# Program order and paced softmax steps in the attention region of a hybrid decoder trunk

## The chip, the cores and the metric

The kernel runs on one core of a Trainium2 chip. The metric is the device time of one execution in microseconds (us). TensorE (PE in the profile) multiplies matrices, VectorE (DVE), ScalarE (ACT) and GpSimd (POOL) do the element-wise work, and SyncE (SP) issues nearly all DMA transfers. Each engine works through its own queue of instructions in order, and semaphores order the engines against each other. An instruction that waits at the head of its queue holds all that stand behind it.

## The reference

Two layers over 1024 tokens of width 1024, in float32. Each layer modulates and normalizes its input, projects it once, gives the columns to three groups of heads, gates each group's output, projects back and adds to the input. The group that the change touches is A, the sliding-window attention; B is a chunked retention, C a gated linear attention.

```python
h = rms_norm(x, pre_gain) * (1.0 + scale) + shift
proj = h @ w_in
(aq, ak, av, ag, rq, rk, rv, rg, gq, gk, gv, gg, ga) = jnp.split(proj, IN_SPLITS, axis=-1)
aq = apply_rotary(aq.reshape(B, S, ATTN_HEADS, HEAD_DIM), positions, rope_freq)
ak = apply_rotary(ak.reshape(B, S, ATTN_KV_HEADS, HEAD_DIM), positions, rope_freq)
a_out = sliding_window_attention(aq, ak, av, sinks) * jax.nn.silu(ag)
...
y = jnp.concatenate([a_out, r_out, g_out], axis=-1) @ w_out
return x + gate * rms_norm(y, post_gain)
```

Attention has 8 query heads of 64 and 2 key/value heads; each query sees the 128 keys up to its own, so a block of 128 queries needs its own block of keys and the one before:

```python
s = jnp.where(valid[None, :, None, None], s, -1e30)
p = jax.nn.softmax(jnp.concatenate([s, sink], axis=-1), axis=-1)[..., :-1]
o = jnp.einsum('bnhgqk,bnkhd->bnqhgd', p.astype(v.dtype), vv)
```

## The kernel before

The tokens lie in eight tiles of 128. Products of full precision are split: each operand becomes a high part in a fast float32 format and a low part (the rest), and three passes (`PASSES`) of matmuls add high by high, high by low and low by high. Weights come as chunks of 128 x 512 in staging tiles (`st`), and are converted on the chip into high and low parts in a large tile (`arena`) by the function `load`; in the last layer the output weights are combined first (`sw_first`, `sw_split`, lines 568 to 603), since the last output projection uses sums of weight blocks (W00, T1, W11, W10 and others).

*Two kinds of order.* A planner in Python writes the program. It keeps a model of PE's clock (`clk`), which each matmul advances. Work beside the stream of projection matmuls is written as generators (jobs). A job yields either a delay on that clock, mostly out of the table `L` by a key (`lat("aq4", l)`; keys with `@1` are for layer 1), or the name of a flag it needs; `pump`, called between pieces of matmuls, lets every job run whose time has come. The whole trunk stands under `tc.manual_schedule(engines={PE})`: PE executes in the order in which the program is written. The other four engines' order is set by a scheduler, with hints: `tc.high_priority()`, and `tc.issue_after(x)`, which keeps what it encloses behind instruction x.

*Pools.* Temporaries `t` (`t2`) of 128 x 512: 10 buffers; staging tiles: 5; score tiles `smx` (128 x 8 x 129, the 129th column for the sink): 3; PSUM: 3 banks `mm`, 5 banks `aux`. A new tile waits until the last reader of the buffer's earlier tile is done.

*The attention region of a layer.* After the projections of B and C the stream projects keys and values (`do_kv`, a pair of token tiles each; job `attn_kv`, L846), the queries (`attn_rot`, L859, twice per half of the tokens: rotary products with tables that it loads, sums L875/L876, copy L881 and four shifted copies by DMA into `mx`), and then the gate (units ag0 and ag1; `gate`, L1671: tanh on ScalarE L1674, product on VectorE L1675, store to `gS` in DRAM). Along with these run the attention blocks, one job `attn_q` (L952) per 128 queries, started by `attn_run`:

1. `attn_split` (L908): q into high and low parts (ScalarE L913, VectorE L914). For block t+1 it is written behind the scores of block t.
2. scores: 24 matmuls into four `aux` banks.
3. `soft` (L917): copies of the previous block's scores (ScalarE), masked copies of the own block's (VectorE L925), the maximum (L927), eight exponentials with sums (ScalarE L930), the reciprocal (L933), the scaling of all rows (GpSimd L935).
4. `turn` (L938): transposes on VectorE (L940), a difference of values (L943) and four masked products on GpSimd (L948, tile `pr`).
5. AV products: 40 small matmuls (fewer in block 0) into four `aux` banks. They are written after the scores of block t+1 (`("sc", l, t + 1)`) and 17.0 us by the planner's clock after step 3.
6. Eviction: four copies on VectorE (L1011) into a `t` tile, with a store to `aoS`. `turn` of block t+1 is written inside this step, behind the last copy.
7. Once the gate of the half is there: loads of `aoS` and `gS` (key "lao"), the product (VectorE L1030), its split (a cast, VectorE L152, and the difference, GpSimd L1037) and stores to `mixS`; in the last layer the later blocks go to `mixF` whole. Helper lines: L166 matmul, L181 transpose, L150 ScalarE copy, L152 VectorE cast, L155 DMA on SP.

In the same stretch jobs convert output weights (`loader`, L476; chunks L527/L528 and L537), and a job computes the next layer's modulation by products of `w_mod` rows (`mod_third`, L366/L368 into `acc`). The weight loader keeps up to `LAG + 1` chunks in flight: it yields 1.2 us after each issue or conversion.

SP issues all of these transfers from one queue, in the scheduler's order.

## Time and profile before

| | us |
|---|---|
| median of 3 runs | 1026.82 (1024.66 to 1029.02) |
| the profiled execution | 1028.49 |
| its span, first to last instruction | 1026.7 |
| PE busy | 961.7 (94% of the span) |
| VectorE busy | 710.1 (69%) |
| ScalarE busy | 378.5 (37%) |
| GpSimd busy | 278.4 (27%) |
| mean clock granted to TensorE | 0.967 |

The span leaves out what lies before the first and behind the last instruction, 1.8 us here. Busy time is averaged over stages that have different limits; a row of a timeline gives start, duration, engine, line, operation, tiles written <- read, how many instructions it stands for, and in brackets the idle time before it with what released it. A row of the waits gives the waiting engine and line, the engine and line waited for, the total, the number of waits and the longest. The clock granted to TensorE is a share of full speed.

### The profile page before, as it was taken

How to read it: one execution, taken by the hardware profiler on the slowest of the kernel's cores; microseconds unless marked ns; L12 is line 12 of the kernel's file. 1: busy time of each engine (PE TensorE's matmuls, PEld its weight loads, DVE VectorE, ACT ScalarE, POOL GpSimd, SP SyncE). 2: the span in 40 equal slices, each digit the busy share in tenths (PEclk: the TensorE clock that was granted, in tenths of full speed). 3: DMA queues.
4: the chain of work that ended last, by engine and by line, in shares of the span. 5: the costliest groups of instructions: out<-in, count | busy, mean ns of one | idle time of the engine just before them, and what ended most of it. 6: DMA issues, size and time to landing. Idle time of an engine off the chain costs nothing. (4 is left out here: it accounts for less than half of the span.)

```text
span 1026.7 us, 21283 instructions
## 1 busy us (share of the span) xinstructions
PE 961.7 (94%) x7965; PEld 833.2 (81%) x7965; DVE 710.1 (69%) x1692; ACT 378.5 (37%) x1088; POOL 278.4 (27%) x319
## 2 busy tenths in 40 slices
PE   5899999999999997797999999999999998988996
PEld 1699999888988875575889999988998887766775
DVE  3889857687657886564488276774775586777876
ACT  2576312234314443322355232133332344454221
POOL 2322011233211254341114101122331043556200
PEclk8899999999999999799999999999999998988999
DMA  9743414433453447787646151351234334697884
GB/s 316 278 134 123 128 43 149 130 112 97 132 167 97 135 137 233 213 240 273 217 129 195 51 166 37 113 170 63 73 110 136 112 102 129 221 288 237 271 277 138
DMA packets 115527, 163.58 MB, mean 159 GB/s; under 512 B 13232, under 2 KB 56796, under 8 KB 115424
## 3 DMA queue, kind: packets, MB, share of 16 engines
q1 hardware_dynamic: 109728, 152.66, 47.4%
q10 hardware_dynamic: 5696, 9.56, 2.5%
q8 instruction: 63, 1.03, 0.4%
q14 instruction: 40, 0.33, 0.1%
HBM read 118.66 MB, written 41.42 MB: 156 GB/s over the span
## 5 line engine op out<-in xcount | busy, mean ns | idle before, releaser
L166 PE MATMUL mm<-arena 128*128 128x256 f32 (+2 forms) x1824 | 300.1, 321 | 1.8 <-ACT arena L708 1.5
L166 PE MATMUL mm<-arena,arena 128*128 128x256 f32 (+2 forms) x1824 | 296.3, 317 | 0.0
L166 PEld LDWEIGHTS mm<-arena 128*128 128x128 f32 x1824 | 259.7, 193 | 25.7 <-ACT arena L708 1.8
L166 PEld LDWEIGHTS mm<-arena,arena 128*128 128x128 f32 x1824 | 254.7, 189 | 24.0 <-issue 2.2
L639 POOL TENSOR_TENSOR sm<-sm,mhalf 128x1 f32<-128x1 f32 (+1 forms) x64 | 55.7, 870 | 332.2 <-DVE sm L638 324.1
L166 PE MATMUL mm<-arena,mx 128*128 128x512 f32 (+1 forms) x564 | 134.9, 395 | 5.0 <-DMA mx<-mixS 3.1
L166 PEld LDWEIGHTS mm<-arena,mx 128*128 128x128 f32 x564 | 103.3, 192 | 30.6 <-issue 3.6
L150 ACT ACTIVATE arena<-st 128x512 fp32r<-128x512 f32 x94 | 55.6, 627 | 65.0 <-PE mm L166 30.8
L537 POOL TENSOR_TENSOR arena<-st,arena 128x512 fp32r<-128x512 f32 x31 | 43.5, 1406 | 119.2 <-ACT arena L150 108.1
L930 ACT ACTIVATE smx<-smx,sm 128x129 f32<-128x129 f32 x128 | 49.7, 390 | 40.9 <-DVE sm L927 40.9
L537 DVE TENSOR_TENSOR arena<-st,arena 128x512 fp32r<-128x512 f32 x77 | 57.7, 770 | 4.0 <-ACT arena L150 2.8
L368 DVE SCALAR_TENSOR_TENSOR acc<-st,c_act,acc 128x512 f32<-128x512 f32 x60 | 47.2, 787 | 16.4 <-DMA st<-in_w_mod_dram 15.9
L181 PE MATMUL aux<-c_ident,t 128*128 128x128 f32 (+1 forms) x292 | 48.9, 285 | 9.1 <-DVE t L670 8.8
L948 POOL TENSOR_TENSOR pr<-smx,c_dmask 32x256 f32<-32x256 f32 x56 | 44.6, 797 | 35.3 <-DVE smx L940 28.4
L166 PE MATMUL aux<-kT,t 64*128 64x256 f32 (+1 forms) x384 | 33.5, 316 | 20.1 <-DVE t L1011 14.6
L935 POOL TENSOR_TENSOR smx<-smx,sm 128x1024 f32<-128x1024 f32 x16 | 31.6, 1976 | 75.2 <-DVE sm L933 56.9
L166 PEld LDWEIGHTS aux<-kT,t 64*128 64x128 f32 x384 | 28.7, 214 | 26.9 <-DVE t L1011 16.6
L181 PEld LDWEIGHTS aux<-c_ident,t 128*128 128x128 f32 (+1 forms) x292 | 35.2, 145 | 17.1 <-DVE t L670 11.7
L150 ACT ACTIVATE t<-aux 128x256 fp32r<-128x256 f32 (+2 forms) x60 | 25.3, 447 | 63.3 <-PE aux L181 63.2
L166 PEld LDWEIGHTS aux<-t,mx 32*128 32x128 f32 (+1 forms) x896 | 39.5, 187 | 3.8 <-issue 2.1
L702 ACT ACTIVATE t<-aux,mod,mod 128x128 f32<-128x128 f32 x68 | 25.9, 460 | 43.2 <-PE aux L181 14.8
L1063 ACT ACTIVATE t<-aux 128x256 f32<-128x256 f32 x32 | 12.3, 383 | 78.4 <-PE aux L166 71.1
(225 smaller groups left out, 1414.0 us busy)
## 6 DMA issues: line engine op xcount, KB each, us to landing
st<-in_w_in_dram SPq DMA_DIRECT2D x96, 256.0 KB, 3.9
st<-in_w_mod_dram SPq DMA_DIRECT2D x64, 256.0 KB, 3.1
mx<-mixS SPq DMA_DIRECT2D x20, 512.0 KB, 5.7
st<-in_w_last_dram SPq DMA_DIRECT2D x36, 256.0 KB, 3.3
mixS<-t SPq DMA_DIRECT2D x64, 128.0 KB, 1.9
mixS<-t SPq DMA_DIRECT2D x26, 256.0 KB, 3.5
wm<-in_w_mod_dram SPq DMA_DIRECT2D x12, 512.0 KB, 5.4
t<-in_x_dram SPq DMA_DIRECT2D x24, 256.0 KB, 5.4
```

The source lines that it names most:

```text
L150: A.activation(dst, src, AF.Copy)
L166: T.matmul(dst, lhsT, rhs, start=start, stop=stop)
L181: T.transpose(dst, src, idn)
L368: V.scalar_tensor_tensor(acc, wt, c_act[:, k:k + 1], acc, ALU.mult, ALU.add)
L537: e.tensor_tensor(lo, st, f(hi), ALU.subtract)
L639: G.tensor_tensor(r, r, mhalf[:, :w], ALU.pow)
L702: A.activation(hf[:, ks], at[kt], AF.Identity, scale=gain, bias=shift)
L930: A.activation(sm[:, h, :], sm[:, h, :], AF.Exp, bias=mx[:, h:h + 1], accum_out=sums[:, h:h + 1])
L935: eng("pn").tensor_tensor(ph, ph, rs.unsqueeze(2).to_broadcast((P, 8, P)), ALU.mult)
L948: eng(f"pr{i}").tensor_tensor(pr[rr], pb[rr, :, i, :], dmask[rr].unsqueeze(1).to_broadcast((32, 8, 32)), ALU.mult)
L1063: A.activation(sq, po, AF.Square)
```

## The change

It has five parts.

1. From `do_kv(2)` to the last gate projection of each layer the program now stands in an inner `tc.manual_schedule(engines=ORDERED)`, with VectorE, ScalarE, GpSimd and SP: there these engines too execute in the order in which the program is written. `one[0]` tells the functions that they are inside. The hints have no say there; `issue_after` around the gate product is left away inside, those around the rotary tables and `turn` altogether.
2. `soft` becomes `masked`, `exps` and `normed`, each written after a pause (3.8 and 3.9 us of the planner's clock, then 2.4). `turn` follows in the block's own job as soon as the previous block's AV products are written, and no longer inside the eviction; the AV products come 5.4 us after it and no longer wait for the next block's scores. `attn_split` of the next block is written behind `masked`.
3. The AV eviction writes into the block's own score tile (its first four head slots) and not into a `t` tile; its store is written 2.4 us later.
4. Weight chunks: inside, the loader yields 2.0 us per step (`LD`), and the modulation's product is written 4.0 us after its load instead of at once.
5. Smaller pauses (the head norms' and the import of `nullcontext` are left out of the diff): the rotary tables are loaded once per half (`attn_tab`) and not once per unit; the sums and the copies become a job (`attn_swap`) with pauses of 2.4 and 1.4; the gate is a job with 2.0 before its store; the store of v stands behind the rotary step of k; the head norms of B and C yield 2.6 between statistics and product; the gate product's stores come 3.2 behind it.

PE's order stays as the planner writes it. In the new file the lines are shifted: masks L939, maximum L941, exponentials L947, reciprocal L953, scaling L955, transposes L960, masked products L968, eviction L1035, gate product L1052, its difference L1058, gate L1700/L1701, modulation L371.

```diff
--- before.py
+++ after.py
...
@@ -159,6 +159,7 @@
 
 
     clk = [0.0]
+    one = [False]
     jobs = []
     flags = {}
 
@@ -362,11 +363,14 @@
             for k in range(KT):
                 wt = stage()
                 dma("lwm", wt, w_mod[l, j, hh, :, k, :])
+                if one[0]:
+                    yield lat("mod2", l)
                 if k == 0 and j < 2:
                     V.tensor_scalar(acc, wt, c_act[:, k:k + 1], None, ALU.mult)
                 else:
                     V.scalar_tensor_tensor(acc, wt, c_act[:, k:k + 1], acc, ALU.mult, ALU.add)
-                yield lat("mod2", l)
+                if not one[0]:
+                    yield lat("mod2", l)
             yield lat("mod3", l)
             pm = aux()
             if j < 2:
@@ -482,10 +486,10 @@
                 while flying and sum(len(s) for _, s in flying) + n > LAG + 1:
                     convert()
                 flying.append((conv, issue()))
-                yield lat("ld1", l)
+                yield LD if one[0] else lat("ld1", l)
             else:
                 convert()
-                yield lat("ld2", l)
+                yield LD if one[0] else lat("ld2", l)
         loading[0] = False
 
     loading = [False]
@@ -846,25 +850,25 @@
     def attn_kv(l, t, pk):
         kr = t1()[:, 0:P]
         v = gp.tile([P, P], F32, tag="va", name=nm("va"), bufs=2)
-        i = A.activation(v, pk[:, 128:256], AF.Copy)
-        if t in (2, 6):
-            kv["at"] = i
-        dma("sv", vS[t], v)
+        A.activation(v, pk[:, 128:256], AF.Copy)
         rotary(kr, pk[:, 0:128], 2, t, 0)
         yield lat("kv1", l)
+        dma("sv", vS[t], v)
         pt = aux()
         transp(pt[:, 0:P], kr, ident)
         split(kv["kT"][0][:, t * P:(t + 1) * P], kv["kT"][1][:, t * P:(t + 1) * P], pt[:, 0:P])
         flag(("kT", l, t), lat("kv2", l))
 
-    def attn_rot(l, hf, g, w_):
-
-
+    def attn_tab(hf):
         sn, cs = t2(), t2()
         for s, d in ((0, sn), (1, cs)):
-            with tc.issue_after(kv["at"].ins):
-                nc.sync.dma_start(d.rearrange("p (s n) -> p s n", s=2),
-                                  tabS[2 * hf:2 * hf + 2, :, s, :].rearrange("s p n -> p s n"))
+            nc.sync.dma_start(d.rearrange("p (s n) -> p s n", s=2),
+                              tabS[2 * hf:2 * hf + 2, :, s, :].rearrange("s p n -> p s n"))
+        return sn, cs
+
+    def attn_rot(l, hf, g, w_, tab):
+
+        sn, cs = tab
         u, w = [t2(), t2()], [t2(), t2()]
         for c in range(2):
             pm = mm()
@@ -872,17 +876,27 @@
             V.tensor_tensor(u[c], pm, cs, ALU.mult)
             V.tensor_tensor(w[1 - c], pm, sn, ALU.mult)
             pump()
+        if g == 0:
+            kv[hf] = mix_tile(F32).rearrange("p a k q -> p (a k q)").rearrange("p (k n) -> p k n", k=4)
+        job(attn_swap(l, hf, g, u, w))
+
+    def attn_swap(l, hf, g, u, w):
+
         V.tensor_tensor(u[0], u[0], w[0], ALU.subtract)
         V.tensor_tensor(u[1], u[1], w[1], ALU.add)
-        if g == 0:
-            kv[hf] = mix_tile(F32).rearrange("p a k q -> p (a k q)").rearrange("p (k n) -> p k n", k=4)
+        if one[0]:
+            yield 2.4
         for j in range(2):
             q = kv[hf][:, 2 * g + j]
             A.activation(q, u[j], AF.Copy)
+        if one[0]:
+            yield 1.4
+        for j in range(2):
+            q = kv[hf][:, 2 * g + j]
             for r in range(2):
                 dst, src = 64 * r + 32 * (1 - j), 64 * r + 32 * j
                 dma("qst", q[dst:dst + 32], u[1 - j][src:src + 32])
-        flag(("q", l, hf, g), lat("aq6", l))
+        flag(("q", l, hf, g), lat("aq6", l) - (3.8 if one[0] else 0.0))
 
     def attn_v(p):
 
@@ -914,7 +928,7 @@
             eng("qsl").tensor_tensor(qs[1], qt, f(qs[0]), ALU.subtract)
         kv["qs"][t] = qs
 
-    def soft(t, n, pss, sm):
+    def masked(t, n, pss, sm):
 
         for g in range(2):
             for r in range(2):
@@ -925,10 +939,16 @@
                 V.copy_predicated(sv, curmask.unsqueeze(1).to_broadcast((P, 2, P)), pv[:, :, n // P - 1, :])
         mx = small(8)
         V.tensor_reduce(mx, sm, AX.X, ALU.max, negate=True)
+        return mx
+
+    def exps(sm, mx):
         sums = small(8)
         for h in range(8):
             A.activation(sm[:, h, :], sm[:, h, :], AF.Exp, bias=mx[:, h:h + 1],
                          accum_out=sums[:, h:h + 1])
+        return sums
+
+    def normed(sm, sums):
         rs = small(8)
         V.reciprocal(rs, sums)
         ph = sm[:, :, 0:128]
@@ -970,23 +990,28 @@
                         mult(pss[g][r][:, j * n:(j + 1) * n], qs[a][rr, 2 * g + j], kv["kT"][b][rr, cols],
                              i == 0, i == 2, n / 4600.0)
         flag(("sc", l, t))
-        if t + 1 < NT and flags.get(("q", l, (t + 1) // 4, 1), 1e9) <= clk[0]:
-            attn_split(t + 1)
         if t % 4 == 3:
             flag(("s", l, t // 4))
         with tc.high_priority():
-            soft(t, n, pss, sm)
-            if t == 0:
-                turn(t, sm)
-        kv["sm"] = sm
+            mx = masked(t, n, pss, sm)
+        if t + 1 < NT and flags.get(("q", l, (t + 1) // 4, 1), 1e9) <= clk[0]:
+            attn_split(t + 1)
+        yield lat("ax1", l)
+        with tc.high_priority():
+            sums = exps(sm, mx)
+        yield lat("ax2", l)
+        with tc.high_priority():
+            normed(sm, sums)
+        yield lat("ax3", l)
+        if t:
+            yield (0.0, ("av", l, t - 1))
+        with tc.high_priority():
+            turn(t, sm)
+        flag(("tn", l, t))
         pb = sm[:, :, 0:128].rearrange("p h (j b) -> p h j b", j=4)
         cur, prev = kv[("v", t // 2)], kv[("v", max(t - 1, 0) // 2)]
         tc_, tp = t % 2, (t - 1) % 2
         yield lat("aq4", l)
-        if t + 1 < NT:
-            yield (0.0, ("sc", l, t + 1))
-        if t:
-            yield (0.0, ("tn", l, t))
         vd, pr = kv["m"] if t else (None, None)
         po = [aux() for _ in range(4)]
         for s in range(5 if t else 4):
@@ -1004,20 +1029,17 @@
                         w_ = cur[rr, 4 * tc_ + j, cc] if j < i or t == 0 else prev[rr, 4 * tp + j, cc]
                         x = pb[rr, r:8:2, j, :]
                     mult(d3, w_, x, s == 0, s == (4 if t else -i % 4 if i < 2 else 3), 0.03)
-        ao = t2()
-        av = ao.rearrange("p (h q) -> p h q", h=4)
+        av = sm[:, 0:4, 0:128]
         with tc.high_priority():
             for i in range(4):
                 last = V.tensor_copy(av[:, :, 32 * i:32 * i + 32], po[i][:, 0:128].rearrange("p (h a) -> p h a", h=4))
-            if t + 1 < NT:
-                with tc.issue_after(last.ins):
-                    turn(t + 1, kv["sm"])
-                flag(("tn", l, t + 1), 0.0)
         kv["ev"] = last
         flag(("av", l, t))
-        dma("sao", aoS[t], av)
         if t in (2, 4):
             attn_v(t // 2 + 1)
+        if one[0]:
+            yield 2.4
+        dma("sao", aoS[t], av)
         yield (0.0, ("av", l, min(t + 1, NT - 1)))
         for k in range(4):
             yield (0.0, ("g", l, t // 4, k))
@@ -1026,17 +1048,21 @@
         for d, src in ((av, aoS), (gt.rearrange("p (k q) -> p k q", k=4), gS)):
             dma("lao", d, src[t])
         yield lat("ag1", l)
-        with tc.issue_after(kv["ev"].ins):
+        with nullcontext() if one[0] else tc.issue_after(kv["ev"].ins):
             V.scalar_tensor_tensor(ao, gt, 0.5, ao, ALU.mult, ALU.mult)
             whole = l == DEPTH - 1 and t >= PLAIN
-            if whole:
-                dma("sm0", mixF[t, :, 0:4, :], av)
-            if not whole or t % 2 == 0:
+            split_ = not whole or t % 2 == 0
+            if split_:
                 mh, ml = t2(F32R), t2(F32R)
                 copy("mg", mh, ao)
                 eng("mgl").tensor_tensor(ml, ao, f(mh), ALU.subtract)
-                for a, m in ((0, mh), (1, ml)):
-                    dma(f"sm{a}", mixS[t, :, a, 0:4, :], f(m).rearrange("p (k q) -> p k q", k=4))
+        if one[0]:
+            yield 3.2
+        if whole:
+            dma("sm0", mixF[t, :, 0:4, :], av)
+        if split_:
+            for a, m in ((0, mh), (1, ml)):
+                dma(f"sm{a}", mixS[t, :, a, 0:4, :], f(m).rearrange("p (k q) -> p k q", k=4))
         for k in range(4):
             flag(("mix1", l, t, k), lat("lay1", l))
 
...
@@ -1659,13 +1687,11 @@
         do_kv(0)
         do_gv(3)
         do_kv(1)
+        tab = attn_tab(0)
         for g in range(2):
-            attn_rot(l, 0, g, used(l, f"aq{g}"))
+            attn_rot(l, 0, g, used(l, f"aq{g}"), tab)
             pump()
         job(attn_run(l))
-        for p in range(2, NP_):
-            do_kv(p)
-        load(l, "ag0")
         mx = {}
 
         def gate(g, hf, kk, pm):
@@ -1673,35 +1699,43 @@
             th = t2()
             A.activation(th, pm, AF.Tanh, scale=0.5)
             V.scalar_tensor_tensor(th, th, 1.0, pm, ALU.add, ALU.mult)
+            yield 2.0
             dma("sg", gS[4 * hf:4 * hf + 4, :, k].rearrange("t p q -> p t q"), th.rearrange("p (t q) -> p t q", t=4))
             flag(("g", l, hf, k), lat("ag2", l))
 
...
+        one[0] = True
+        with tc.manual_schedule(engines=ORDERED):
+            do_kv(2)
+            do_kv(3)
+            load(l, "ag0")
+            tab = attn_tab(1)
             for g in range(2):
+                attn_rot(l, 1, g, used(l, f"aq{g}"), tab)
+                pump()
+                if l == DEPTH - 1 and g == 0:
+                    sw_first("W00")
+                else:
+                    load(l, ("o3", "ag1")[g])
+            for hf in range(2):
+                for g in range(2):
+                    for kk in range(2):
+                        pm = mm()
+                        project_T(pm, l, hf, used(l, f"ag{g}"), kk * P)
+                        job(gate(g, hf, kk, pm))
+                        pump()
+                    if hf and not g:
+                        if l == DEPTH - 1:
+                            sw_first("W10")
+                        else:
+                            load(l, "o2")
+                if not hf:
                     if l == DEPTH - 1:
+                        sw_first("T1")
+                        sw_first("W11")
                     else:
+                        load(l, "o0")
+                        load(l, "o1")
+        one[0] = False
@@ -1743,8 +1777,10 @@
...
-L = {
...
-"aq4": 17.0,
...
-"aq4@1": 17.0,
...
+L = {
...
+"ax1": 3.8, "ax1@1": 3.8, "ax2": 3.9, "ax2@1": 3.9, "ax3": 2.4, "ax3@1": 2.4, "aq4": 5.4,
...
+"aq4@1": 5.4,
...
 CHUNK = 7
+LD = 2.0
+ORDERED = {mybir.EngineType.DVE, mybir.EngineType.Activation, mybir.EngineType.Pool, mybir.EngineType.SP}
 LAG = 2
 FIN = 1
 
```

More of the change, by code (lines that the diff above doesn't have):

```diff
@@ L1 @@
 import math
-from contextlib import ExitStack
+from contextlib import ExitStack, nullcontext
 import numpy as np
@@ L1066, in head_norm_gate @@
         r = rstd_of(ss, 4, scale, eps)
+        if one[0]:
+            yield 2.6
         g1 = t1()
@@ L1069, in head_norm_gate @@
         eng("hng").tensor_tensor(g1, g1, gate, ALU.mult)
-        yield lat("hn1", l)
+        yield lat("hn1", l) - (2.6 if one[0] else 0.0)
         pt = aux()
```

25 lines of the change are left out of this document (1 added, 24 removed).

## The prediction

> **What bounds the kernel now.** I read the engines' busy time first, then stretches of 50 us, then the tensor engine's waits by line, then the single instructions around each wait. The page:
>
> ```profile
> PE 961.7 (94%) x7965; PEld 833.2 (81%) x7965; DVE 710.1 (69%) x1692; ACT 378.5 (37%) x1088; POOL 278.4 (27%) x319
> ```
>
> PE is the bound, with 65 us of idle time (1026.7 - 961.7). The stretches (start:end, then busy time of PE, PEld, DVE, ACT, POOL, the clock granted to TensorE, DMA share, GB/s) show where that idle time is:
>
> ```profile
> 350.00:400.00 50.00, 44.01 (x448) 35.05 (x448) 36.80 (x65) 22.44 (x76) 20.37 (x19) 0.96 0.54 164
> 400.00:450.00 50.00, 38.94 (x403) 30.82 (x402) 36.05 (x60) 17.85 (x69) 26.05 (x25) 0.83 0.78 226
> ...
> 850.00:900.00 50.00, 44.70 (x461) 35.05 (x449) 34.26 (x63) 22.86 (x79) 24.35 (x24) 0.91 0.57 182
> 900.00:950.00 50.00, 41.18 (x326) 32.11 (x326) 38.04 (x59) 22.89 (x76) 30.57 (x27) 0.85 0.84 264
> 950.00:1000.00 50.00, 48.04 (x272) 37.28 (x271) 40.37 (x73) 14.92 (x33) 7.23 (x8) 0.97 0.83 275
> ```
>
> The attention region of layer 0 lies at about 318 to 436 us, that of layer 1 at about 815 to 945, so the change touches just the stretches with idle time. What PE waited for, first between 355 and 440, then between 855 and 990:
>
> ```profile
> PE aux L166 <- DVE t L1011: 7.0, 3, 4.0
> PE aux L166 <- ACT t L913: 5.6, 1, 5.6
> PE aux L166 <- DVE smx L925: 4.5, 2, 4.3
> ```
>
> ```profile
> PE aux L166 <- DVE t L1011: 11.7, 4, 4.1
> PE aux L166 <- DVE smx L925: 2.4, 2, 1.2
> PE mm L166 <- DVE t L1435: 1.9, 1, 1.9
> ```
>
> Layer 0 loses 7.0 + 5.6 + 4.5 = 17.1 us, layer 1 loses 16.0, of which 4.1 is its last wait on L1011 and 1.9 the output stage. So 10.0 lies before that. PE stands for the copy that clears the AV banks (L1011), the masks that clear the score banks (L925) and the split of q (L913): VectorE's and ScalarE's queues, not their load.
>
> A stall also costs clock. The loss in a stretch is busy time times (1 - clock). Layer 0: 44.01 x 0.04 + 38.94 x 0.17 = 8.4 us, 0.49 per us of idle time. Layer 1: 44.70 x 0.09 + 41.18 x 0.15 + 48.04 x 0.03 = 11.6 us over 16.0, 0.73 per us. I price a microsecond of stall at 1.49 us in layer 0 and 1.73 in layer 1.
>
> What stands in front of L1011? PE's stalls and, below, VectorE's instructions around them:
>
> ```profile
> 398.94 1.43 PE L166 MATMUL aux<-kT,t 64*128 64x256 f32 x14 [4.00 <-DVE t L1011]
> ...
> 432.08 0.58 PE L166 MATMUL aux<-kT,t 64*128 64x256 f32 x1 [5.58 <-ACT t L913]
> 433.66 1.22 PE L166 MATMUL aux<-kT,t 64*128 64x256 f32 x8 [1.00 <-DVE t L1011]
> ```
>
> ```profile
> 943.16 1.22 PE L166 MATMUL aux<-arena,mx 128*128 128x512 f32 x2 [4.14 <-DVE t L1011]
> ```
>
> ```profile
> 397.27 0.75 DVE L528 SCALAR_TENSOR_TENSOR arena<-st,gnc,arena 128x512 fp32r<-128x512 f32 x1 [4.19 <-ACT arena L527]
> ...
> 398.60 0.88 DVE L1011 COPY t<-aux 128x128 f32<-128x128 f32 x4
> ...
> 401.13 1.90 DVE L1030 SCALAR_TENSOR_TENSOR t<-t,t 128x512 f32<-128x512 f32 x2
> 402.95 0.91 DVE L152 CAST t<-t 128x512 fp32r<-128x512 f32 x1
> 403.79 1.18 DVE L1030 SCALAR_TENSOR_TENSOR t<-t,t 128x512 f32<-128x512 f32 x1
> 404.90 1.52 DVE L152 CAST t<-t 128x512 fp32r<-128x512 f32 x1
> ```
>
> ```profile
> 429.15 0.69 DVE L1030 SCALAR_TENSOR_TENSOR t<-t,t 128x512 f32<-128x512 f32 x1 [3.70 <-issue]
> 429.76 1.22 DVE L927 TENSOR_REDUCE sm<-smx 128x8 f32<-128x1032 f32 x1
> 430.90 0.42 DVE L152 CAST t<-t 128x512 fp32r<-128x512 f32 x1
> ```
>
> ```profile
> 940.76 0.69 DVE L603 TENSOR_TENSOR st<-st,st 128x512 f32<-128x512 f32 x1 [3.88 <-DMA st<-in_w_last_dram]
> ...
> 942.82 0.88 DVE L1011 COPY t<-aux 128x128 f32<-128x128 f32 x4
> ```
>
> Each time a step whose data had not come stood at the head of VectorE's queue: a weight piece (4.19 and 3.88 us), a gate product (3.70, with the reduction that the exponentials need behind it). The change orders these queues by hand, so it decides what stands there next.
>
> **The change, part by part** (line numbers of before). Durations of the steps, between 300 and 480 us:
>
> ```profile
> L930 ACT ACTIVATE smx<-smx,sm 128x129 f32<-128x129 f32 x64 | 24.9, 390 | 27.2 <-DVE sm L927 27.2
> L948 POOL TENSOR_TENSOR pr<-smx,c_dmask 32x256 f32<-32x256 f32 x28 | 22.0, 784 | 19.3 <-DVE smx L940 16.3 <-DVE smx L957 1.4
> ...
> L368 DVE SCALAR_TENSOR_TENSOR acc<-st,c_act,acc 128x512 f32<-128x512 f32 x16 | 14.4, 899 | 7.8 <-DMA st<-in_w_mod_dram 7.5
> ...
> L925 DVE COPY_PREDICATED smx<-c_curmask,aux 128x256 f32<-128x256 int32 x32 | 11.9, 439 | 2.0 <-ACT smx L150 1.8
> ...
> L1037 POOL TENSOR_TENSOR t<-t,t 128x512 fp32r<-128x512 f32 x8 | 11.3, 1416 | 14.2 <-DVE t L152 10.3 <-DVE t L1030 2.8 <-issue 0.6
> ...
> L940 DVE STREAM_TRANSPOSE smx<-smx 128x1024 f32<-128x1024 f32 x8 | 9.9, 1238 | 4.3 <-POOL smx L935 4.3
> ```
>
> Weight pieces converted 2.0 us per step, and the modulation product 4.0 us after its load: this removes the wait of the first kind. By the emitted order two or three steps, 4 to 6 us, now lie between issue and conversion. Against the landing times of the page
>
> ```profile
> st<-in_w_in_dram SPq DMA_DIRECT2D x96, 256.0 KB, 3.9
> ...
> st<-in_w_mod_dram SPq DMA_DIRECT2D x64, 256.0 KB, 3.1
> ...
> st<-in_w_last_dram SPq DMA_DIRECT2D x36, 256.0 KB, 3.3
> ```
>
> that is enough while SP's queue is short. The stall of 4.00 at 398.94 goes, and with it the 7.5 us in which VectorE waited for modulation loads, which cost PE nothing where no L1011 was behind.
>
> The eviction into the score tile frees one of ten temporaries per block; L913 had waited for such a slot. It holds the score tile until its store has landed, some microseconds that three such tiles cover; its copies stay (0.88 for four). The store now reads pieces of 512 bytes; no row shows such a store, so I bound it between nothing and one landing of a plain one, and take nothing, since the product that reads it back comes a block later. Rotary tables loaded once per half save four loads per layer on SP, which hide beside projections. The later stores (v, gate, mix) and the pieces of the head norm cost nothing on PE as long as 3 to 7 us of projection matmuls stand before the reader; without that cover each would cost its added pause, 2.0 to 3.2.
>
> Now the new order, block by block. After the last transposes a block needs 1.24 + 4 x 0.78 = 4.4 us before its AV products; the plan gives 5.4, so 1.0 is spare.
>
> Layer 0. AV(4): three gate products with casts (3 x (0.69 + 0.42) = 3.3 on VectorE) and three splits on GpSimd (3 x 1.42 = 4.3) now stand between the q split of block 6 and the transposes and diagonal products of block 4. The GpSimd work starts a cast later than VectorE's, so the delay is 1.1 + 4.3 - 1.0 = 4.4 if nothing stretches, 3.3 - 1.0 = 2.3 if GpSimd's part falls beside other work, 6 if they stretch as in the rows at 401 to 405; I take 5. Scores(7): the second half of AV(5)'s eviction stands behind the reciprocal of block 6, which needs its reduction (1.2) and eight exponentials (8 x 0.39 = 3.1), and the reduction stands behind a weight cast that waits for its load. That is at least 3 us and at most what it was (5.58 + 1.00); I take 5.5. AV(1) and AV(5): one or two steps of 0.7 stand ahead, about 1.1 each. Sum 12.7 against 17.1: -4.4 x 1.49 = -6.6 us.
>
> Layer 1. The price of PE's cover, from the page's groups:
>
> ```profile
> L166 PE MATMUL mm<-arena,mx 128*128 128x512 f32 (+1 forms) x564 | 134.9, 395 | 5.0 <-DMA mx<-mixS 3.1
> ```
>
> Scores(3): a gate product waits for its tanh on ScalarE behind block 2's exponentials (3.1, half of it covered): 1.6. AV(2): by the emitted order twelve matmuls of 512 columns lie between scores(3) and it, where twenty-four did, 2.9 us for 5.7 (0.24 each, 134.9 us by 564); the transposes stand behind four masks (1.8), a reduction (1.2), a split and a weight step (0.7 each), so 4.4 + 4.4 - 2.9 = 5.9 at most, 2.8 if half of the front work is done by then; I take 4.5. Scores(6): the eviction of block 4 stands behind the sum of a T1 weight pair that is issued twelve such matmuls, 2.9 us, ahead, with six loads of 256 KB for gate products in front on SP, and behind three gate products (3.3). The loads cost their issue and bandwidth: 3 us late is the least (nearest row: 3.88 at 940.76, the same kind of wait), 9 the most; I take 6.5. AV(1) and AV(5): 0.9 and 0.7. Sum 14.2 against 10.0: +4.2 x 1.73 = +7.3 us.
>
> Output stage. SP's load for a gate product of block 3 waits for a temporary that scores(6) frees, and the weight loads and mix stores behind it wait too; the first output tile and the combined weights come later. Before, PE lost 4.14 there; between the same and 9 us after; I take 2.5 more: +4.3 us.
>
> Sum -6.6 + 7.3 + 4.3 = +5.0 on the profiled execution's 1028.49 us, 1033.5, so 1033. The median of the runs shown is 1.7 below that execution, within their spread of 4.4, and I do not shift for it.
>
> **A rule against the change.** In the rows at 401 to 405 a cast took 0.91 and 1.52 us and a product 1.18, where the group's plain ones take 0.42 and 0.69; GpSimd was splitting beside them. The Trainium skill, page SBUF — State Buffer, section "SBUF: two separate sides", says that VectorE and GpSimd share a port pair as an exclusive lock, and the loser waits for the whole instruction; the trace agrees as far as those durations go. By that rule a hand-made order that sets product, cast and split of three tiles in a row would serialize them wherever they stand.
>
> **Rivals.**
> - The pacing works. For it: the three longest waits above are each one late datum, and the new pauses exceed its landing time. Against it: the bunches of three gate products remain. At the lower ends layer 0 keeps 2.3 + 3 + 1.5 = 6.8 of 17.1, -15.3 us, and layer 1 stays where it is, the output too: 1013. It decides if the T1 pair lands before block 4's eviction is due.
> - SP's queue becomes the bound of layer 1. Fixed order on SP lets one load without a slot hold every weight load behind it. For it: SP already moves 264 GB/s at 900 to 950. At the upper ends layer 1 is at 0.9 + 1.6 + 5.9 + 9 + 0.7 = 18.1, +14.0 us, the output at +4.9, +8.4, layer 0 unchanged: 1051.
> - Serialized products: AV(4) costs 10 instead of 5, and the bunch before scores(6) 2.2 more: 1033 + 5 x 1.49 + 2.2 x 1.73 = 1044. For it the rows at 401 to 405, against it that other casts in the region took 0.42.
> - Nothing moves: PE's order is nearly the same and what layer 0 wins layer 1 gives back, with the output stage's delay covered by matmuls of layer 1's first tiles: 1028.
>
> **How the numbers follow.** Forecast (1033, alone 1029 to 1039) 0.34, pacing works 0.34, SP bound 0.13, serialized 0.09, nothing moves 0.10. About 5 us (0.5%) is what a measurement of this kernel can tell from no change, so from 1021.7 to 1031.9 counts as the same. Faster: the pacing rival 0.33 and little else; same: 0.09 of nothing moves and some 0.08 of the forecast's lower part; slower: the rest, 0.50. The range leaves out 0.1 on each side: 1010 to 1049. Cases of both signs hold much, so the forecast's own range stands above.
>
> **What would show it.** Right: no PE wait over 2 us before the scores of block 4 of layer 0; waits of about 5 before AV(4) and scores(7), released by POOL and by L1035 of the new code; in layer 1 waits of 4 to 6 before AV(2) and scores(6), the latter with VectorE idle on a load of the last layer's weights; a clock near 0.9 at 850 to 950. Wrong: if layer 1 shows no VectorE idle on weight loads and PE busy above 47 of 50 us there, the pacing rival holds; if SP is held for 5 us or more by a temporary and PE stands in the output stage, the SP rival.

## The result and the profile after

The changed kernel takes 1055.3 us in the median of 4 runs (1053.2 to 1059.0), the kernel before 1026.0 (1024.7 to 1029.0) beside it: a ratio of 1.0285, 95% interval 1.0248 to 1.0322. It is 29 us slower. The prediction had 1033, with a range to 1049. The profiled execution is the longest of the four (1059.0), as the one before was near the upper end of its own.

The page of the changed kernel, engines:

```profile
PE 972.0 (92%) x7965; PEld 837.2 (79%) x7965; DVE 700.0 (66%) x1692; ACT 378.8 (36%) x1088; POOL 278.6 (26%) x319
```

The span grew from 1026.7 to 1057.2. PE's idle time (span less busy time) went from 65.0 to 85.2 us, and the same matmuls took 10.3 us longer (961.7 to 972.0), at a mean granted clock of 0.952 for 0.967. VectorE has even less to do than before. Stretches of 50 us, in the columns of before:

```profile
350.00:400.00 50.00, 44.99 (x457) 35.23 (x456) 29.25 (x61) 22.37 (x76) 19.86 (x21) 0.93 0.44 129
400.00:450.00 50.00, 32.08 (x291) 24.22 (x290) 31.98 (x55) 17.48 (x57) 24.29 (x25) 0.70 0.70 212
...
850.00:900.00 50.00, 43.97 (x479) 33.76 (x480) 29.34 (x61) 21.39 (x75) 21.96 (x22) 0.93 0.34 100
900.00:950.00 50.00, 36.51 (x327) 27.48 (x325) 31.29 (x56) 19.95 (x72) 25.21 (x25) 0.89 0.76 251
950.00:1000.00 50.00, 42.46 (x304) 32.77 (x304) 40.17 (x58) 16.33 (x32) 22.70 (x17) 0.87 0.77 252
```

The loss sits at 400 to 450 (PE busy 7 us less than before, clock 0.70 for 0.83) and spreads over 900 to 1000 (5 and 6 us less in the two rows). What PE waited for, from 340 to 460:

```profile
PE aux L167 <- issue: 9.7, 1, 9.7
PE mm L167 <- POOL arena L541: 5.0, 1, 5.0
PE aux L167 <- DVE smx L960: 3.8, 1, 3.8
PE aux L167 <- DVE smx L1035: 3.4, 1, 3.4
PE aux L167 <- POOL pr L968: 0.8, 2, 0.4
```

From 840 to 940:

```profile
PE aux L167 <- DVE smx L1035: 6.1, 1, 6.1
PE mm L167 <- ACT arena L150: 5.3, 2, 5.0
PE aux L167 <- POOL pr L968: 2.0, 4, 0.7
PE aux L167 <- issue: 0.6, 1, 0.6
```

And from 940 to the end:

```profile
PE mm L167 <- DMA mx<-mixS: 5.5, 3, 3.9
PE mm L167 <- DMA ma<-mixS: 5.5, 1, 5.5
PE mm L167 <- DMA a<-mixS: 2.4, 2, 1.9
PE mm L167 <- DVE t L1463: 1.6, 1, 1.6
PE aux L167 <- DVE smx L1035: 0.6, 1, 0.6
```

That is 22.7, 14.0 and 15.6 us, where the kernel before lost 17.1, 10.0 and 6.0. Before, PE stood for evictions and masks. Now it also stands for weight halves (L541, L150) and, in the output stage, for transfers.

The longest wait, 9.7 us, ends at 437.07 with the AV products of block 5 in layer 0. The profile names no releaser for it ("issue"); the transposes that these products read end at 436.97. PE, then VectorE, then SP's issues around it:

```profile
437.07 1.31 PE L167 MATMUL aux<-smx,vx 32*64 32x128 f32 x12 [9.72 <-issue]
```

```profile
420.26 0.19 DVE L953 RECIPROCAL sm<-sm 128x8 f32<-128x8 f32 x1
435.06 0.75 DVE L371 SCALAR_TENSOR_TENSOR acc<-st,c_act,acc 128x512 f32<-128x512 f32 x1 [14.61 <-DMA st<-in_w_mod_dram]
435.73 1.24 DVE L960 STREAM_TRANSPOSE smx<-smx 128x1024 f32<-128x1024 f32 x1
```

```profile
401.97 1.01 SPq L155 DMA_DIRECT2D st<-in_w_out_dram  x2
414.24 0.33 SPq L155 DMA_DIRECT2D st<-in_w_mod_dram  x1
419.15 0.33 SPq L155 DMA_DIRECT2D st<-in_w_out_dram  x1
419.53 0.42 SPq L155 DMA_DIRECT2D gS<-t  x1
420.00 4.12 SPq L155 DMA_DIRECT2D mixS<-t  x6
424.22 0.56 SPq L155 DMA_DIRECT2D st<-in_w_out_dram  x1
424.88 2.91 SPq L155 DMA_DIRECT2D vx<-vS  x5
428.11 0.35 SPq L155 DMA_DIRECT2D st<-in_w_mod_dram  x1
```

VectorE stood 14.6 us at a modulation product, with the transposes of block 5 behind it. Its load went out at 428.11, because SP had issued nothing for 11 us up to 414.24 and for 4.5 us up to 419.15, and then had a backlog of stores and v loads to get rid of. SP's waits in those two gaps:

```profile
SPq L155 <- DVE acc L371: 7.6, 1, 7.6
SPq L155 <- DMA st<-in_w_mod_dram: 3.6, 1, 3.6
```

```profile
SPq L155 <- POOL arena L541: 4.5, 1, 4.5
```

For 7.6 and 4.5 us SP waited for staging tiles that VectorE (L371, behind three gate products) and GpSimd (L541, behind the masked products) had yet to give back. It is a circle: a compute queue holds a tile, SP holds the loads behind the one that needs it, and the compute queue then holds at a load that SP has not issued. The tables of waits show the circle in this place; whether SP's order is the cause is a matter for the runs.

### The profile page after: what moved, and what is told of

It is laid out like the page before. It is cut to its first block, busy times and chain, and to the rows that moved or that the text cites. A ratio compares the mean times of both kernels' runs of the same rounds, so it can differ in the third digit from the quotient of the medians.

```text
span 1057.2 us, 21252 instructions
## 1 busy us (share of the span) xinstructions
PE 972.0 (92%) x7965; PEld 837.2 (79%) x7965; DVE 700.0 (66%) x1692; ACT 378.8 (36%) x1088; POOL 278.6 (26%) x319
## 5 line engine op out<-in xcount | busy, mean ns | idle before, releaser
L167 PE MATMUL mm<-arena,arena 128*128 128x256 f32 (+2 forms) x1824 | 300.0, 319 | 5.4 <-ACT arena L150 5.3
L167 PE MATMUL mm<-arena,mx 128*128 128x512 f32 (+1 forms) x564 | 137.6, 400 | 9.2 <-DMA mx<-mixS 7.6
L150 ACT ACTIVATE arena<-st 128x512 fp32r<-128x512 f32 x94 | 57.3, 628 | 75.8 <-DMA st<-in_w_in_dram 20.4
L371 DVE SCALAR_TENSOR_TENSOR acc<-st,c_act,acc 128x512 f32<-128x512 f32 x60 | 47.1, 785 | 27.2 <-DMA st<-in_w_mod_dram 26.8
L955 POOL TENSOR_TENSOR smx<-smx,sm 128x1024 f32<-128x1024 f32 x16 | 31.4, 1964 | 124.2 <-DVE sm L953 105.2
L541 POOL TENSOR_TENSOR arena<-st,arena 128x512 fp32r<-128x512 f32 x31 | 42.0, 1355 | 81.1 <-ACT arena L150 77.8
L541 DVE TENSOR_TENSOR arena<-st,arena 128x512 fp32r<-128x512 f32 x77 | 57.5, 761 | 4.1 <-ACT arena L150 2.6
L968 POOL TENSOR_TENSOR pr<-smx,c_dmask 32x256 f32<-32x256 f32 x56 | 46.1, 823 | 42.4 <-DVE smx L960 33.0
L947 ACT ACTIVATE smx<-smx,sm 128x129 f32<-128x129 f32 x128 | 49.6, 390 | 14.0 <-DVE sm L941 13.9
L182 PEld LDWEIGHTS aux<-c_ident,t 128*128 128x128 f32 (+1 forms) x292 | 35.2, 145 | 18.2 <-DVE t L674 12.6
L150 ACT ACTIVATE t<-aux 128x256 fp32r<-128x256 f32 (+2 forms) x60 | 25.3, 448 | 63.3 <-PE aux L182 63.2
L150 ACT ACTIVATE smx<-aux 128x256 f32<-128x256 f32 x56 | 18.4, 384 | 65.5 <-PE aux L167 46.8
L167 PE MATMUL aux<-t,mx 32*128 32x32 f32 (+1 forms) x896 | 40.7, 272 | 0.0
```

The costliest lines, as they stand in the source:

```text
L150: A.activation(dst, src, AF.Copy)
L167: T.matmul(dst, lhsT, rhs, start=start, stop=stop)
L182: T.transpose(dst, src, idn)
L371: V.scalar_tensor_tensor(acc, wt, c_act[:, k:k + 1], acc, ALU.mult, ALU.add)
L541: e.tensor_tensor(lo, st, f(hi), ALU.subtract)
L947: A.activation(sm[:, h, :], sm[:, h, :], AF.Exp, bias=mx[:, h:h + 1], accum_out=sums[:, h:h + 1])
```

## The experiments

Each ratio is against runs of the kernel before beside it; 0.01 is about 10 us. Theory 1: the fixed order costs, SP's (1a) or that of the compute engines, with SP in their wake (1b). Theory 2: the paces cost. Theory 3: the bunch of gate products costs. Later on, theory 1c: SP's order costs only together with the paces. The first runs leave the changed kernel's program as it is and free one engine or more from the program's order.

**SP free.**

```diff
-ORDERED = {DVE, Activation, Pool, SP}
+ORDERED = {DVE, Activation, Pool}
```

> VectorE, ScalarE and GpSimd keep the program's order, SP's queue is the scheduler's again. If SP's fixed order is what makes the loads late (theory 1a): the wait of 9.7 us before the AV products of block 5 in layer 0 and the waits on mix tiles in the output stage go, 15 to 20 us less, about 1037. If the late loads come from the engines that free their buffers (theory 1b): within 5 us of 1055.

Measured 1043.0 us, ratio 1.0191 (1.0149 to 1.0233): 10 to 12 us back, less than theory 1a had and more than 1b. The wait of 9.7 is 3.3:

```profile
427.59 1.67 PE L167 MATMUL aux<-smx,vx 32*64 32x128 f32 x44 [3.30 <-issue]
```

The two waits of 5.0 on gate weights stayed, and against the forecast most of the waits on mix tiles in the output stage did too (9.4 of 13.4 us).

**VectorE free**, and **ScalarE and GpSimd free** (each with the others ordered):

```diff
-ORDERED = {DVE, Activation, Pool, SP}
+ORDERED = {Activation, Pool, SP}   # the second run: {DVE, SP}
```

> VectorE's order is the scheduler's, the other three keep the program's. Theory 1b (VectorE's head of line is what PE feels: a modulation product without its load stands in front of the transposes of block 5): 1030 to 1042, the wait of 9.7 us falls under 4. Theory 1a (SP): 1048 or more, since the loads come as late as before.

> ScalarE's and GpSimd's orders are the scheduler's. The two waits of 5.0 us on the gate weights (a low half on GpSimd behind the masked products of block 2 in layer 0, a copy on ScalarE behind the exponentials of block 3 in layer 1) go if their order is the cause: 10 us of idle time and some 6 of clock, about 1040. If they come from the pace of the loader: within 5 us of 1055.

Measured 1056.5 (1.0321; 1.0273 to 1.0369) and 1059.4 (1.0346; 1.0311 to 1.0382): nothing back. With ScalarE and GpSimd free the waits on gate weights did go, but waits of 8.7 and 4.8 us for transposes came in their place. In these two runs, with SP held, what was removed turned up elsewhere.

**All free (paces only)**, and **only SP ordered**.

```diff
-ORDERED = {DVE, Activation, Pool, SP}
+ORDERED = {PE}                     # the second run: {SP}
```

> All paces and parts of the change stay, but the inner region names only TensorE, which is in the program's order anyway, so the scheduler orders VectorE, ScalarE, GpSimd and SP. Theory 1 (the fixed order is the cost; freeing SP alone gave back 12 of 29 us, freeing the others without SP nothing, since a held SP queue sets their data): 1020 to 1035 us. Theory 2 (the paces are the cost): 1040 or more, like the run with SP free.

> Only SP keeps the program's order, the three compute engines are the scheduler's. Theory 1a (SP's order is what costs): 1035 to 1045, above the run with paces only by about 12. Theory 1b (the compute engines' order costs, and SP only in their wake): within 5 us of the run with paces only.

Measured 1039.2 (1.0130; 1.0100 to 1.0160) and 1054.6 (1.0269; 1.0231 to 1.0308). The first lies between its two forecasts, the second 10 us above both of its own. The paces and pieces cost 13 us without any order, and SP's order on top of them 14. The order of the three compute engines on top of that (1.0285) adds nothing that can be measured. With SP free it may add some 6 (1.0191 against 1.0130); the intervals just overlap.

**SP's order on the kernel before**, with no other part of the change:

```diff
+        with tc.manual_schedule(engines={SP}):
             for p in range(2, NP_):
                 do_kv(p)
...
```

> The kernel before, with one thing of the change: in the attention region SP keeps the program's order; no pace, no softmax piece and no other engine's order is touched. Theory 1a (SP's fixed order costs by itself; with all paces it was 1054.6 against 1039.2): about 15 us above before, 1036 to 1044. Theory 1c (SP's order costs only with the paces, which set when loads are written): within 5 us of before.

Measured 1052.7, ratio 1.0247 (1.0223 to 1.0272): 25 us from SP's order alone, without a pace, a piece or another engine's order. Theory 1a stands, at more than the 15 it had, and 1c falls. The 25 and the 13 of the paces and pieces do not add up: both together cost 27 (1.0269), so they overlap. How far SP runs ahead shows in its issues of output-weight loads between 300 and 400 us: before, changed, and this run:

```profile
st<-in_w_out_dram SPq DMA_DIRECT2D x16, 256.0 KB
```

```profile
st<-in_w_out_dram SPq DMA_DIRECT2D x8, 256.0 KB, 3.5
```

```profile
st<-in_w_out_dram SPq DMA_DIRECT2D x7, 256.0 KB, 5.7
```

The scheduler had issued 16 loads of 256 KB by 400 us, the program's order 7 or 8. The others fall into the busiest part, with the gate loads and mix stores. With paces only it is 14, with all ordered but SP 9. The same count in layer 1 (loads of the last layer's weights from 815 to 900 us) is 19 before, 8 in the changed kernel and 6 in this run, and over the runs, those with earlier loads (below) left out, it goes with the time: 6 to 9 in those of 1053 to 1059 us, 11 to 15 in those of 1043 to 1046, 16 to 20 in those of 1025 to 1039. That is no proof of a cause, since a kernel that is late has also come less far by 900. PE's waits in this run are not at one place; they are more of the old kinds. From 840 to the end:

```profile
PE aux L166 <- DVE t L1011: 16.7, 5, 4.6
PE mm L166 <- DVE t L1435: 5.4, 2, 4.7
PE mm L166 <- DMA mx<-mixS: 2.7, 2, 1.9
```

**Stores off SP.** Is it that SP's stores wait for their producers, in front of loads?

```diff
-"sg": "S", "sao": "S", "sm0": "S", "sm1": "S", "sv": "S"
+"sg": "A", "sao": "A", "sm0": "A", "sm1": "A", "sv": "A"
```

> As the run of the kernel before with SP in program order (1052.7 us), but the stores of the attention region that wait for a producer (v, gate, AV output, gate product) go out from ScalarE's queue, which the scheduler orders; the loads stay on SP in program order. If SP's order costs because such stores stand ahead of loads: 1028 to 1038. If it costs because of the loads' own waits for buffers (staging tiles, temporaries, v tiles): 1045 or more.

Measured 1042.7, ratio 1.0163 (1.0127 to 1.0200), between the two forecasts: about 8 of 25 us went, some 17 stay. Not all of the 17 need be the loads', since ScalarE now stands at the stores, here 4.7 us for the product that a gate store sends (L1676), with a weight copy (L527) behind it:

```profile
ACT arena L527 <- DVE t L1676: 4.7, 1, 4.7
```

**Earlier loads.** Would the head start, written into the program, give the rest back?

```diff
+            if l == DEPTH - 1:
+                sw_first("T1")
+                sw_first("W11")
+            else:
+                load(l, "o0")
+                load(l, "o1")
             for hf in range(2):
...
-                if not hf:
...
```

> As the run of the kernel before with SP in program order (1052.7 us), with the requests for two units of output weights written ahead of the gate projections, where they stood behind the first half of them. If SP's order costs because the scheduler had issued those loads far ahead of their place in the program: 1035 to 1043, with 11 or more output-weight loads issued between 300 and 400 us. If the head start is not the cause: 1048 or more.

> The same with the producer-bound stores on ScalarE's queue as well. If head start and waiting stores are the two parts of SP's cost and add up: 1026 to 1034. If they are one cost seen twice: about 1040.

> The changed kernel, all four orders fixed, with the same two requests written earlier. If lost head start is what SP's order takes from it: 1040 to 1048. If the fixed order of the compute engines then puts conversions in front of softmax steps instead: 1052 or more.

Measured 1067.5 (1.0416; 1.0388 to 1.0444), 1049.7 (1.0252; 1.0223 to 1.0281) and 1050.2 (1.0249; 1.0227 to 1.0271). These give no verdict. The two units lie in the places of the first half's normalized input, which the gate projections of that half still read; with the requests moved ahead of them, these projections work on weights and wait for their conversion, a wait that belongs to none of the theories. In the first of the three:

```profile
914.16 2.08 PE L166 MATMUL mm<-arena,arena 128*128 128x512 f32 x4 [8.09 <-POOL arena L568]
```

That a lost head start is the rest of SP's cost fits the counts and is not shown; the order may as well cost through loads that stand waiting for buffers.

**The loader's pace**, in the changed kernel, in the changed kernel with SP free, and the other way round (1.2 to 2.0) in the kernel before, inside the region only:

```diff
-LD = 2.0
+LD = 1.2
```

> The loader's pace inside goes back from 2.0 to 1.2 us, the order stays fixed. If the two waits of 5.0 us before gate matmuls come from the pace (theory 2): both go, 10 us of idle time and 6 of clock, about 1040, less what earlier conversions hold up on VectorE. If they come from what stands ahead on GpSimd and ScalarE (theory 1): within 5 us of 1055, or up to 15 slower, because pieces are then converted with their loads still on the way.

> The changed kernel with both: SP free and the loader at 1.2 us; VectorE, ScalarE and GpSimd keep the program's order. If SP's order (12 us) and the pace (10 us) are separate costs: about 1033. If they are one cost seen twice (late loads): 1040 to 1045. Whether the fixed order of the three compute engines costs something by itself shows in what is left above before.

> The kernel before, with the loader's pace in the attention region at 2.0 instead of 1.2 us and nothing else. Theory 2 (the pace makes weights late for the gate projections): 5 to 15 us above before, with waits on weight halves before gate matmuls. Else, if the pace only hurts where the fixed order stands behind it: within 5 us of before, or below it, since pieces then have 2 us more to land.

Measured 1045.5 (1.0184; 1.0153 to 1.0215), 1039.0 (1.0124; 1.0091 to 1.0157) and 1026.4 (0.9999; 0.9977 to 1.0020). The pace costs nothing in the kernel before, where the scheduler orders the queues, and 10 us where the program does. But the gain is not the removal of one kind of wait: at 1.2 both waits of 5.0 changed (one went, in place of the other there is one of 6.5 on another weight half), and the place of the longest wait got worse. SP issued 11 output-weight loads by 400 us for 8, so the pace may act through the head start.

```profile
428.42 1.99 PE L167 MATMUL aux<-smx,vx 32*64 32x128 f32 x61 [19.14 <-issue]
```

Whether the gains of SP's freedom and of the pace add up is not settled: added, the ratios give 1.0090 with an error of some 0.006, and the run with both gave 1.0124.

**Gate products spread.**

```diff
+        if one[0] and 0 < t < 4:
+            yield (0.0, ("la", l, t - 1))
+        flag(("la", l, t), 6.0)
         ao, gt = t2(), t2()
```

> The gate products of blocks 1 to 3 are let go 6.0 us apart by the planner's clock, where the change emits three or four together as soon as the half's gate is there; all else is as in the changed kernel. If the bunch holds up the transposes and evictions behind it and, through staging tiles, SP (theory 3): the waits of 3.8 before the AV products of block 4 in layer 0 and of 6.1 before the scores of block 6 in layer 1 go, the one of 9.7 falls too, 1035 to 1045. If the bunch is not the cause: within 5 us of 1055.

Measured 1053.8 (1.0263; 1.0237 to 1.0290), not to be told from the changed kernel. The waits that I had put down to the bunch did fall (3.8 to 0.8, 6.1 to 3.9), yet the one of 9.7 only to 8.2, and the output stage kept its own. Theory 3 explains two waits and not the time: 1.5 us by the medians, within the noise.

**The parts that are not order**, on the kernel before: the eviction into the score tile with the shared tables, and the late modulation product.

```diff
-        ao = t2()
-        av = ao.rearrange("p (h q) -> p h q", h=4)
+        av = sm[:, 0:4, 0:128]
...
+        if g == 0:
+            sn, cs = t2(), t2()
...
```

> The kernel before, with the AV eviction into the score tile and the rotary tables loaded once per half, and nothing else. If these parts are neutral, as the prediction had them: within 5 us of before. If the store in pieces of 512 bytes or the longer hold of a score tile costs: 5 or more above; if the freed temporaries help: up to 8 below.

```diff
                 dma("lwm", wt, w_mod[l, j, hh, :, k, :])
+                if one[0]:
+                    yield lat("mod2", l)
...
```

> The kernel before, with only the modulation's product written 4.0 us behind its load inside the region. If a product that waits for its load at VectorE's head is a cost: 2 to 6 us below before. If the scheduler keeps it out of the way already: within 3 us of before.

Measured 1029.7 (1.0027; 1.0008 to 1.0045) and 1025.2 (0.9999; 0.9978 to 1.0021): some 3 us, and nothing.

**Without any order**: the hint on the gate products restored, and the region left unmarked, so that only the softmax pieces, the eviction, the tables and the small job changes remain.

```diff
-        with nullcontext() if one[0] else tc.issue_after(kv["ev"].ins):
+        with tc.issue_after(kv["ev"].ins):
```

> As the run with paces only (1039.2 us, no engine's order fixed), with the hint restored that keeps the gate products behind the AV eviction. If the missing hint lets gate products stand ahead of the eviction on VectorE (the wait of 16.6 us before the scores of block 6 in layer 1): that wait falls under 5, 1028 to 1033. If not: within 3 us of 1039.

```diff
-        one[0] = True
+        one[0] = False
```

> No engine's order is fixed and the region is not marked, so loader pace, modulation product, hint and stores are as before; the softmax in pieces with its own transposes, the eviction into the score tile and the shared tables remain. If the pieces cost (the transposes are no longer tied to the eviction): 1035 or more. If the marked region's paces and the missing hint cost: 1027 to 1033.

Measured 1039.4 (1.0139; 1.0100 to 1.0177) and 1035.0 (1.0090; 1.0058 to 1.0122). The hint is not the cause: the wait of 16.6 us that the run with paces only has before the scores of block 6 in layer 1 stayed, 17.0 with the hint. The row of the run with paces only:

```profile
913.30 1.01 PE L167 MATMUL aux<-kT,t 64*128 64x256 f32 x6 [16.61 <-DVE smx L1035]
```

Of the 13 us without order about 3 are the eviction and the tables, some 6 the pieces and the small job changes (1.0090 less 1.0027), and perhaps 4 the marked region's paces (1.0130 less 1.0090, intervals that overlap). What within the pieces costs was not taken apart. The traces give a hint: PE waits 40.4 us for the eviction (L1035) with paces only and 24.2 with the pieces alone, 18.7 before (L1011), and in the place of the wait of 16.6 VectorE runs the next block's transposes in front of it, where they used to be written behind its last copy:

```profile
902.87 1.25 DVE L960 STREAM_TRANSPOSE smx<-smx 128x1024 f32<-128x1024 f32 x1 [1.79 <-POOL smx L955]
...
912.96 0.87 DVE L1035 COPY smx<-aux 128x128 f32<-128x128 f32 x4
```

No run put them back behind it.

No version beat the kernel before; the loader's pace alone and the late modulation product alone equal it.

## Why the prediction was wrong

The direction was right, the size was not. Two steps failed: SP's fixed order was not priced (about 14 of the 27 to 29 us, by the run with only SP ordered against the one with no order), and the paces and softmax pieces were taken to cost nothing by themselves (the other 13). By its own steps:

- *PE is the bound, and stalls cost 1.49 to 1.73 us each with the clock.* Right for this pair: idle time grew by 20.2 us, the span by 30.5, which is 1.51. It is no fixed price: by the profiles it lies between 0.74 (paces only: 13.5 more idle, 10.0 more span) and 1.68 (ScalarE and GpSimd free: 18.2 and 30.5) over the runs that are 9 us or more longer than before.
- *"Weight pieces converted 2.0 us per step ... that is enough while SP's queue is short."* This is the first step that failed. The condition was written down and not priced. The wait of 4.00 before the scores of block 4 did go. But SP's queue was not short: VectorE waited 14.6 us for one modulation load, and behind it PE's wait of 9.72 came. I counted steps between issue and conversion in the program's order, and took the issue to happen at its place. In the kernel before, the scheduler had issued 16 output-weight loads by 400 us, here SP had issued 8.
- *AV(4) 5, scores(7) 5.5 in layer 0.* Right in place: 3.8 (with 0.8 for masked products) and 3.4. *AV(5) 1.1*: 9.7, by the step above. A wait of 5.0 on the low half of a gate weight, which GpSimd's order had put behind masked products, was not seen at all. Sum 22.7 for 12.7.
- *Scores(6) 6.5 in layer 1*: 6.1, with the weight pair and the gate products in front of the eviction, as told. But what VectorE stood at in front was no late load: it was a weight copy that ScalarE had behind eight exponentials (the row below), so the sign named for it did not come. *AV(2) 4.5*: a wait of 5.0 is there, but for a weight copy that stood behind exponentials on ScalarE. Scores(3): none. Sum 14.0 for 14.2, partly by luck.

```profile
913.96 0.69 DVE L572 TENSOR_TENSOR arena<-st,arena 128x512 fp32r<-128x512 f32 x1 [3.21 <-ACT arena L150]
```

- *Output stage +2.5*: +9.6, twice the upper end. The mechanism came as told: SP stood 9.7 us, to 923.75, at a load for a gate product, until PE (the scores of block 6) freed a temporary, and PE later waited 5.5, 5.5 and 2.4 us for loads of mix tiles. The size was wrong, and SP's order is not all of it: with SP free it stood there 6.1 us, and 9.4 of these 13.4 us stayed; with no order at all 3.1.

```profile
SPq L155 <- PE aux L167: 9.7, 1, 9.7
```

- *The eviction, tables and later stores at nothing, and no term for the softmax in pieces*: this is the second step that failed. With no engine's order fixed, the eviction and the tables cost some 3 us, the pieces and small jobs some 6, the paces perhaps 4. Why the pieces cost stays open.
- *The rival of SP* (1051, a chance of 0.13) named the queue that the runs show: SP's order alone costs 25 us on the kernel before. Its sign came too (SP held 9.7 us by a temporary, PE standing in the output stage). But it left layer 0 unchanged and had 18.1 us for layer 1, where the waits were 22.7 and 14.0, and it had nothing for the paces and pieces, so that 1051 lies near 1055 is in part luck. It looked for single loads without a slot; in the run with SP's order alone PE's waits are spread over the region.
- *The serialized products* did not decide: two casts took 1.40 and 1.37 us, as in the rows before, at a wait of 3.8 and not 10.

```profile
407.36 0.43 DVE L152 CAST t<-t 128x512 fp32r<-128x512 f32 x1
...
408.43 1.40 DVE L152 CAST t<-t 128x512 fp32r<-128x512 f32 x1
...
410.45 1.37 DVE L152 CAST t<-t 128x512 fp32r<-128x512 f32 x1
```

- *The pacing rival* (1013) fell: the waits that the paces should remove were replaced by others of the same size or longer, and the paces and pieces cost 13 us even where SP's order was free.

## What to carry to other kernels

Before an engine that issues transfers is put in program order, count how many loads the scheduler issues ahead of their place (here 16 by 400 us against 7): the order takes this head start away, and here it came with 25 us, though that the head start is what costs was not shown. Price a fixed queue as a whole, by running it alone: one engine's order can carry nearly the whole cost (25 us alone, of 29 for the whole change, although the other parts alone cost 13), while freeing the engines that seem to stall, VectorE or ScalarE and GpSimd here, gives nothing back. Removing a visible wait says little while the queue behind it is held: here waits of 5 us went and others of the same size came.

## What was not expected of the hardware

A microsecond of PE's idle time had no fixed price in clock: the same matmuls took 958.2 us busy with paces only, 961.7 before and 974.0 with ScalarE and GpSimd free, at idle times of 78.5, 65.0 and 83.2 us. These are single traces.

The v loads seem to land later once the AV output is stored from the score tile: the median from issue to landing at 350 to 450 us was 4.4 us before and 6.7 in the run with only that eviction and the tables. But it was 3.9 in the changed kernel with SP free, which stores the same way. So the source of the store is not enough to explain it.

```profile
vx<-vS SPq DMA_DIRECT2D x10, 128.0 KB, 4.4
```

```profile
vx<-vS SPq DMA_DIRECT2D x10, 128.0 KB, 6.7
```

```profile
vx<-vS SPq DMA_DIRECT2D x10, 128.0 KB, 3.9
```

Whether the place of the v loads in the queue slows them was not tried.
